# Gated DeltaNet layer: joins on both column halves, a raised eviction rank, another spread of the gates, outputs turned by VectorE

## The chip, the cores and the metric

The kernel runs on one core of a Trainium2 chip. The metric is the device time of one execution in microseconds (us). The five engines have a queue each and meet by semaphores: TensorE (PE, with its weight loads PEld), VectorE (DVE), ScalarE (ACT), GpSimd (POOL), and SyncE (SP), which issues the DMAs.

## The reference

Four layers over 1024 positions of width 1024, each with RMSNorm, adaLN shift and scale, one input projection that also gives a SiLU gate, a mixer, an output projection and a gated residual. The mixers are HGRN2, sliding-window attention, gated DeltaNet (GDN), HGRN2. All is fp32. The change is in the GDN layer (one helper of the HGRN2 layers is renamed):

```python
def gdn_mixer(h, w_in, w_out, conv_w, a_log, dt_bias, onorm_g):
    qkv, z, a, b = jnp.split(h @ w_in, [GD_QKV, GD_QKV + GD_VW, GD_QKV + GD_VW + GD_V_HEADS], axis=-1)
    qkv = jax.nn.silu(causal_conv(qkv, conv_w))
    ...
    beta = jax.nn.sigmoid(b)
    g = -jnp.exp(a_log) * jax.nn.softplus(a + dt_bias)
    o = gated_delta_scan(q, k, v, beta, g)
    o = rmsnorm(o, onorm_g).reshape(B, T, GD_VW)
    return (o * jax.nn.silu(z)) @ w_out
# gated_delta_scan, for each chunk:
    X = lax.linalg.triangular_solve(A + eye, rhs, left_side=True, lower=True, unit_diagonal=True)
    u, w = X[..., :dv], X[..., dv:]
    v_new = u - w @ S
    o = (q_ * jnp.exp(d)[..., None]) @ S + qk @ v_new
    S = S * jnp.exp(d_last) + (k_ * jnp.exp(d_last - d)[..., None]).T @ v_new
```

There are 8 key heads and 16 value heads of 128. z is the gate, a and b give the decays.

## The kernel before

Activations lie with features on the 128 partitions and time in two halves (hf) of 512. An fp32 operand is split in a high and a low part, and each product is three matmuls (mm3, L195 to L197): hi by hi, lo by hi, hi by lo. proj_fm projects 128 columns so (24 matmuls per half) and gives the PSUM bank to an eviction (evac).

The GDN layer goes by u = 0 to 7, a key head with its two value heads. proj_kq evicts k and q with a short convolution (conv: copy gd_xs L627, first tap L631, three taps on DVE L633, tanh L634, product L635). proj_v does the same for v and turns it with PE (vtr_ps). proj_z evicts the gates (L709, L711) and stores them in the DRAM tensor od[1], where the outputs later stand too. inverse(u) inverts the 16 triangular matrices of 128 of a pair: 62 substitution steps on DVE for blocks of 32 (L766, L767), joins of 32 (z_ps L795, L805, L806), then two joins of 64 (L814, L821), each 16 products of 64 by 64, with copies by ACT and DVE after each. Both joins of 64 take one half of PE's columns: the first puts its results on partitions 64 to 127 (up) of two PSUM banks, the second on 0 to 63 (lo).

scan(u) goes through 8 chunks of 128 in order with the state S: ks_ps (L864, L865), y on DVE (L870), w_ps (L875), ws on ACT (L876) and wg on DVE (L877), the new state (S_ps L881, DVE L887), and the output product w_ps L891, added to ot (L894). After four chunks finish normalizes: it multiplies ot by the factor of each row (L842), turns it in four PE transposes (otr_ps L845), multiplies by the gate loaded from od[1] (L847) and stores it there. out_load later loads the outputs and splits them (o_hi on ACT, o_lo on DVE, L1182, L1183), and out_mm multiplies them by the output weights (outp_ps).

The order of the work is fixed when the program is built. weave merges generators by planned time: for each pair scan(u) and inverse(u+1) lie beside a chain of projections for later pairs, and the table ZL says which gates are projected beside which pair. high_priority ranks instructions within a scheduler that then writes one fixed in-order queue for each engine; burst gives a rank of 4000, which keeps a group of matmuls together. The first inverse has a weave of its own, beside kq of u = 1, v of u = 0 and the second half of u = 0's gates. Ahead of it the first half of the projection for u = 0 runs under early, with a raised rank, while the norm of the second half (hhi L496) is still being made. decays projects a and b with weights gd_wab split in hi and lo, 32 columns each.

Of the kernel before, what the change touches and what calls it, by code (L numbers as in the profile page):

```python
# [10 lines left out]
F32 = mybir.dt.float32  # L11
# [9 lines left out]
P = 128  # L21
T = 1024
# [9 lines left out]
GB = {"k": 5, "q": 4, "kt": 4, "v": 4, "zs": 1, "tmp": 2, "tb": 3, "of": 2, "f256": 4, "ot": 1}  # L32
# [3 lines left out]
EO, EW = 60, 150  # L36
# [10 lines left out]
ZL = ((1, 0, 1), (2, 0, 1)), ((3, 0, 1),), ((4, 0, 1),), ((5, 0),), ((5, 1),), ((6, 0, 1),), ((7, 0, 1),), ()  # L47
# [36 lines left out]
class Trunk:  # L84
    def __init__(self, ctx, tc, ins):
# [8 lines left out]
        self.np_, self.pb, self.pw = 0, 3, 0  # L94
        self.dram = pool("dram", space=bass.MemoryType.DRAM)
        self.xd = self.dram.tile([D, T], F32, name="xd")
        self.od = [self.dram.tile([D * (1 + n), T], F32, name=f"od{n}") for n in range(2)]
        self.hhi, self.hlo = [None, None], [None, None]
# [14 lines left out]
    def early(self, g):  # L113

        self.pw = EW
        with self.tc.high_priority(offset=EO):
            drain(g)
        self.pw = 0
# [14 lines left out]
    def burst(self):  # L133

        return self.tc.high_priority(offset=BURST)

# [363 lines left out]
    def proj_fm(self, w, c0, evac, halves=(0, 1)):  # L500

        w = self.pre.pop(c0, None) or self.load_cols(w, c0)
        for hf in halves:
# [6 lines left out]
            evac(hf, ps)  # L510
# [14 lines left out]
    def gdn(self, i, side):  # L525
# [88 lines left out]
        place = lambda h, hf: self.od[1][h * P:(h + 1) * P, hf * HT:(hf + 1) * HT]  # L614
# [90 lines left out]
        def proj_z(u, dd, halves=(0, 1)):  # L705
            for a in range(2):
                def ev(hf, ps):
                    th = tl("tb")
                    nc.scalar.activation(th, ps, AF.Tanh, scale=0.5)  # L709
                    zs = tl("zs")  # L710
                    nc.vector.scalar_tensor_tensor(zs, th, 1.0, ps, ALU.add, ALU.mult)  # L711
# [762 lines left out]
```

## Time and profile before

| | us |
|---|---|
| runs | 2743.67, 2731.29, 2732.64 |
| median | 2732.64 |
| the profiled execution's own time | 2734.63 |
| span of its profile | 2732.9 |

The profile is of one execution. Its page gives busy times by engine, a chain of work traced back from the end, and the costliest groups of instructions; other views of the trace give single instructions, waits by releaser, and windows. Matmuls run in a pipeline and their ends are modelled, so a matmul's price is read from the spacing of starts, not from its duration. Among the largest groups of the page are, beside the projections, these rows of the GDN layer (busy us, mean ns | idle before them and what ended it):

```profile
L633 DVE SCALAR_TENSOR_TENSOR gd_tb<-gd_xs,taps,gd_tb 128x512 f32<-128x512 f32 x192 | 144.9, 754 | 22.5 <-ACT gd_tb L631 20.1
```

### The profile page before, as it was taken

How to read it: one execution, taken by the hardware profiler on the slowest of the kernel's cores; microseconds unless marked ns; L12 is line 12 of the kernel's file. 1: busy time of each engine (PE TensorE's matmuls, PEld its weight loads, DVE VectorE, ACT ScalarE, POOL GpSimd, SP SyncE). 2: the span in 40 equal slices, each digit the busy share in tenths (PEclk: the TensorE clock that was granted, in tenths of full speed). 3: DMA queues.
4: the chain of work that ended last, by engine and by line, in shares of the span. 5: the costliest groups of instructions: out<-in, count | busy, mean ns of one | idle time of the engine just before them, and what ended most of it. 6: DMA issues, size and time to landing. Idle time of an engine off the chain costs nothing.

```text
span 2732.9 us, 51521 instructions
## 1 busy us (share of the span) xinstructions
PE 2647.5 (97%) x19071; PEld 2133.6 (78%) x19071; DVE 2019.3 (74%) x5714; ACT 1235.5 (45%) x3139; POOL 132.6 (5%) x352
## 2 busy tenths in 40 slices
PE   8999999999999999899999999999999999999999
PEld 4878878778877767677788887788778888887877
DVE  6776766778687877677888898988765857556575
ACT  4333333444454655454456456555543433333342
POOL 0000100000000000001001100100000001000000
PEclk9999999999999999999999999999999999999999
DMA  6332222344223243324343344332553211111133
GB/s 238 97 94 78 67 81 79 113 133 148 65 83 97 91 141 100 110 70 115 101 124 102 97 125 112 103 103 77 151 189 117 78 58 38 55 44 47 46 121 113
DMA packets 347665, 273.29 MB, mean 100 GB/s; under 512 B 68963, under 2 KB 276246, under 8 KB 347414
## 3 DMA queue, kind: packets, MB, share of 16 engines
q1 hardware_dynamic: 347126, 268.95, 32.8%
q8 instruction: 150, 2.46, 0.4%
q14 instruction: 101, 0.83, 0.1%
q0 software_dynamic: 288, 1.05, 0.1%
HBM read 224.77 MB, written 45.15 MB: 99 GB/s over the span
## 4 chain that ended last, share of the span: by engine, by line
PE 73%; DVE 15%; DMA 6%; ACT 3%; issue 2%; SPq 0%; DVEq 0%; ACTq 0%
PE proj_ps L196 10%; PE proj_ps L195 10%; PE proj_ps L197 10%; PE outp_ps L195 4%; PE outp_ps L197 4%; PE outp_ps L196 4%; DMA ada_w<-in_ada_w_dram 3%; PE projt_ps L195 3%; PE projt_ps L197 3%; PE projt_ps L196 3%; DVE w_lo L171 1%; PE pv_ps L1356 1%; DVE gd_tb L633 1%; PE ada_row L391 1%; PE w_ps L875 1%
## 5 line engine op out<-in xcount | busy, mean ns | idle before, releaser
L195 PE MATMUL proj_ps<-hhi,w_hi 128*128 128x512 f32 x1664 | 679.9, 409 | 12.6 <-ACT gd_tb L631 11.4
L197 PE MATMUL proj_ps<-hhi,w_lo 128*128 128x512 f32 x1664 | 680.5, 409 | 0.0
L196 PE MATMUL proj_ps<-hlo,w_hi 128*128 128x512 f32 x1664 | 675.2, 406 | 0.0
L195 PEld LDWEIGHTS proj_ps<-hhi,w_hi 128*128 128x128 f32 x1664 | 316.2, 190 | 71.1 <-ACT gd_tb L631 15.6
L196 PEld LDWEIGHTS proj_ps<-hlo,w_hi 128*128 128x128 f32 x1664 | 315.8, 190 | 58.6 <-issue 2.4
L197 PEld LDWEIGHTS proj_ps<-hhi,w_lo 128*128 128x128 f32 x1664 | 315.9, 190 | 56.4 <-issue 1.0
L170 ACT CAST w_hi<-w_raw 128x512 fp32r<-128x512 f32 x332 | 201.9, 611 | 309.3 <-PE proj_ps L196 195.0
L171 DVE TENSOR_TENSOR w_lo<-w_raw,w_hi 128x512 fp32r<-128x512 f32 x332 | 223.4, 675 | 158.2 <-ACT w_hi L170 132.5
L196 PE MATMUL projt_ps<-w_lo,hhi 128*128 128x256 f32 x896 | 258.7, 291 | 4.7 <-DVE w_lo L171 4.7
L195 PE MATMUL projt_ps<-w_hi,hhi 128*128 128x256 f32 x896 | 257.7, 290 | 0.9 <-ACT w_hi L170 0.9
L197 PE MATMUL projt_ps<-w_hi,hlo 128*128 128x256 f32 x896 | 256.8, 290 | 0.0
L195 PE MATMUL outp_ps<-o_hi,w_hi 128*128 128x512 f32 x576 | 229.2, 400 | 3.8 <-ACT o_hi L1182 2.4
L196 PE MATMUL outp_ps<-o_lo,w_hi 128*128 128x512 f32 x576 | 229.2, 399 | 0.0
L197 PE MATMUL outp_ps<-o_hi,w_lo 128*128 128x512 f32 x576 | 227.9, 398 | 0.8 <-DVE w_lo L174 0.8
L196 PEld LDWEIGHTS projt_ps<-w_lo,hhi 128*128 128x128 f32 x896 | 171.1, 192 | 8.1 <-DVE w_lo L171 6.0
L195 PEld LDWEIGHTS projt_ps<-w_hi,hhi 128*128 128x128 f32 x896 | 171.1, 192 | 4.0 <-ACT w_hi L170 1.3
L197 PEld LDWEIGHTS projt_ps<-w_hi,hlo 128*128 128x128 f32 x896 | 170.8, 192 | 2.3 <-issue 1.0
L633 DVE SCALAR_TENSOR_TENSOR gd_tb<-gd_xs,taps,gd_tb 128x512 f32<-128x512 f32 x192 | 144.9, 754 | 22.5 <-ACT gd_tb L631 20.1
L173 ACT ACTIVATE w_hi<-w_raw,par 128x512 fp32r<-128x512 f32 (+1 forms) x136 | 94.5, 698 | 140.0 <-PE outp_ps L196 98.9
L195 PEld LDWEIGHTS outp_ps<-o_hi,w_hi 128*128 128x128 f32 x576 | 108.8, 189 | 27.7 <-ACT o_hi L1182 3.8
L174 DVE SCALAR_TENSOR_TENSOR w_lo<-w_raw,par,w_hi 128x512 fp32r<-128x512 f32 (+1 forms) x136 | 96.8, 716 | 43.5 <-ACT w_hi L173 42.4
L404 DVE SCALAR_TENSOR_TENSOR ada_acc<-ada_w,par,ada_acc 128x512 f32<-128x512 f32 x140 | 104.5, 746 | 32.4 <-DMA ada_w<-in_ada_w_dram 31.4
(394 smaller groups left out, 4918.9 us busy)
## 6 DMA issues: line engine op xcount, KB each, us to landing
ada_w<-in_ada_w_dram SPq DMA_DIRECT2D x160, 256.0 KB, 2.7
w_raw<-in_hg_in_w_dram SPq DMA_DIRECT2D x136, 256.0 KB, 2.8
w_raw<-in_gd_in_w_dram SPq DMA_DIRECT2D x108, 256.0 KB, 3.1
o_in<-od SPq DMA_DIRECT2D x72, 256.0 KB, 3.2
w_raw<-in_gd_out_w_dram SPq DMA_DIRECT2D x64, 256.0 KB, 2.8
w_raw<-in_sw_in_w_dram SPq DMA_DIRECT2D x48, 256.0 KB, 2.9
w_raw<-in_hg_out_w_dram SPq DMA_DIRECT2D x40, 256.0 KB, 2.8
ada_w<-in_ada_w_dram SPq DMA_DIRECT2D x8, 1024.0 KB, 9.0
```

Source lines behind the costliest of these rows:

```text
L170: nc.scalar.copy(hi, raw)
L171: nc.vector.tensor_tensor(lo, raw, hi.bitcast(F32), ALU.subtract)
L173: nc.scalar.activation(hi, raw, AF.Copy, scale=scale)
L174: nc.vector.scalar_tensor_tensor(lo, raw, scale, hi.bitcast(F32), ALU.mult, ALU.subtract)
L195: mm(out, a[0], b[0], start=start, stop=False)
L196: mm(out, a[0], b[1], start=False, stop=False)
L197: mm(out, a[1], b[0], start=False, stop=stop)
L391: nc.tensor.matmul(pr[0:1, :], self.cT[:, k:k + 1], wk[:, k, :], start=k == 0, stop=k == KT - 1)
L404: self.nc.vector.scalar_tensor_tensor(acc, w, c, acc, ALU.mult, ALU.add)
L633: nc.vector.scalar_tensor_tensor(y, xs[:, j:j + HT], w(j), y, ALU.mult, ALU.add)
L875: nc.tensor.matmul(po[:, hd[a]], dd["u"][a, hf][:, cs], rhs, start=True, stop=True)
L1356: nc.tensor.matmul(po[a * 64:(a + 1) * 64], vg[:, n + 1 - nkb + b, :], p4[:, :, a, :], start=b == 0, stop=b == nkb - 1)
```

## The change

Six things are changed.

- early takes a rank (EV = 300) for the evictions of the first projection.
- decays has the high and low columns of a and b side by side as 64 columns: two matmuls per block in place of three. The two halves of the result are added after the transposes, by an ACT copy and a DVE add. The product lo by lo is now computed too.
- In inverse the joins of 64 go by turns to both column halves of PE, in one bank. Bursts are tied, so that all wait for the first. The joins of 32 are in another order, and two of the four POOL copies stand later.
- The first weave has the projections in another order, with the gates of u = 1, and 72.8 us of planned work; ZL is shifted by one pair.
- finish has no PE transposes and no gate: the multiply by the row's factor writes in a permuted order, a DVE transpose turns blocks of 32 by 32, and four DMAs store the result. The gates have their own DRAM tensor zd and are multiplied in out_load, on DVE.
- In scan wg is computed by ACT, after the S_ps matmuls.

Lines in the changed kernel are 9 to 18 further on (L627 is L644, L766 is L782, L821 is L836, L891 is L906).

**The start of the layer, ACT.** hhi is the normed input of the second half, gd_xs the copy that begins an eviction of the first projections, gd_wab the weights of a and b. Before:

```order
L170 CAST w_hi<-w_raw 128x512
L496 ACTIVATE hhi<-n_t,mod 128x512 x2
L170 CAST w_hi<-w_raw 128x512
L496 ACTIVATE hhi<-n_t,mod 128x512 x2
L627 COPY gd_xs<-proj_ps 128x512
L631 ACTIVATE gd_tb<-proj_ps,taps 128x512
L544 CAST gd_wab<-w_raw 128x256
L627 COPY gd_xs<-proj_ps 128x512
L575 ACTIVATE gd_tmp<-gd_tmp 128x16
```

With the change:

```order
L179 CAST w_hi<-w_raw 128x512
L505 ACTIVATE hhi<-n_t,mod 128x512 x2
L179 CAST w_hi<-w_raw 128x512
L505 ACTIVATE hhi<-n_t,mod 128x512 x2
L644 COPY gd_xs<-proj_ps 128x512
L648 ACTIVATE gd_tb<-proj_ps,taps 128x512
L644 COPY gd_xs<-proj_ps 128x512
L555 CAST gd_wab<-w_raw 128x8x32
L592 ACTIVATE gd_tmp<-gd_tmp 128x16
```

The first eviction stands in the same place; the second has moved ahead of the cast of gd_wab.

**The first inverse, DVE.** L766 and L767 (later L782, L783) are the substitution, one pair for each j. Before, from the fifth pair:

```order
L766 TENSOR_TENSOR gd_tmp<-gd_A,gd_Tb 128x81
L767 TENSOR_TENSOR gd_Tb<-gd_Tb,gd_tmp 128x27x3
L766 TENSOR_TENSOR gd_tmp<-gd_A,gd_Tb 128x78
L677 TENSOR_SCALAR gd_ms<-gd_ms 128x16
L767 TENSOR_TENSOR gd_Tb<-gd_Tb,gd_tmp 128x26x3
L150 TENSOR_SCALAR rs_y<-gd_ms 128x16
L766 TENSOR_TENSOR gd_tmp<-gd_A,gd_Tb 128x100
L152 SCALAR_TENSOR_TENSOR rs_t<-rs_y,gd_ms 128x16
L633 SCALAR_TENSOR_TENSOR gd_tb<-gd_xs,taps,gd_tb 128x512
L767 TENSOR_TENSOR gd_Tb<-gd_Tb,gd_tmp 128x25x4
L153 TENSOR_TENSOR rs_t<-rs_t,rs_y 128x16
L633 SCALAR_TENSOR_TENSOR gd_tb<-gd_xs,taps,gd_tb 128x512
```

With the change, from the second half of the second pair's rows:

```order
L727 SCALAR_TENSOR_TENSOR gd_tb<-gd_tb,proj_ps 128x512
L783 TENSOR_TENSOR gd_Tb<-gd_Tb,gd_tmp 128x30
L782 TENSOR_TENSOR gd_tmp<-gd_A,gd_Tb 128x58
L783 TENSOR_TENSOR gd_Tb<-gd_Tb,gd_tmp 128x29x2
L782 TENSOR_TENSOR gd_tmp<-gd_A,gd_Tb 128x56
L783 TENSOR_TENSOR gd_Tb<-gd_Tb,gd_tmp 128x28x2
L782 TENSOR_TENSOR gd_tmp<-gd_A,gd_Tb 128x81
L783 TENSOR_TENSOR gd_Tb<-gd_Tb,gd_tmp 128x27x3
L782 TENSOR_TENSOR gd_tmp<-gd_A,gd_Tb 128x78
L783 TENSOR_TENSOR gd_Tb<-gd_Tb,gd_tmp 128x26x3
L782 TENSOR_TENSOR gd_tmp<-gd_A,gd_Tb 128x100
L783 TENSOR_TENSOR gd_Tb<-gd_Tb,gd_tmp 128x25x4
```

Taps of convolutions (L633) and the norm of the next k and q (L677, L150 to L154) stood between the steps; now a few evictions of gates (L727) do, and some rows further on weights (w_lo).

**The last scan, PE.** This is behind the last join of 64. proj_ps are the last projections, outp_ps the output projection; S_ps, ks_ps and w_ps are the scan of u = 7. Before, from the second product of its first chunk on:

```order
L875 MATMUL w_ps<-gd_v,gd_uq 128x128
L196 MATMUL outp_ps<-o_lo,w_hi 128x512
L197 MATMUL outp_ps<-o_hi,w_lo 128x512
L195 MATMUL outp_ps<-o_hi,w_hi 128x512
L881 MATMUL S_ps<-gd_ws,gd_kt 128x256
L891 MATMUL w_ps<-gd_wg,gd_uq 128x128 x2
L196 MATMUL outp_ps<-o_lo,w_hi 128x512
L197 MATMUL outp_ps<-o_hi,w_lo 128x512
L864 MATMUL ks_ps<-gd_S,gd_k 128x256
L865 MATMUL ks_ps<-gd_S,gd_q 128x256
```

With the change, the rows from the first new state on:

```order
L895 MATMUL S_ps<-gd_ws,gd_kt 128x256
L906 MATMUL w_ps<-gd_wg,gd_uq 128x128
L206 MATMUL proj_ps<-hhi,w_lo 128x512
L906 MATMUL w_ps<-gd_wg,gd_uq 128x128
L879 MATMUL ks_ps<-gd_S,gd_k 128x256
L880 MATMUL ks_ps<-gd_S,gd_q 128x256
L890 MATMUL w_ps<-gd_y,gd_uq 128x128 x2
L895 MATMUL S_ps<-gd_ws,gd_kt 128x256
L906 MATMUL w_ps<-gd_wg,gd_uq 128x128 x2
L879 MATMUL ks_ps<-gd_S,gd_k 128x256
L880 MATMUL ks_ps<-gd_S,gd_q 128x256
L658 MATMUL vtr_ps<-ident,gd_tb 128x128 x4
```

Before, output rows (outp_ps) stood around the first steps of the scan; now two steps follow each other with transposes of v alone between them. Between the last join and the first outp_ps stand 36 proj_ps rows before, 13 with the change.

The diff, cut where it repeats itself:

```diff
-GB = {"k": 5, "q": 4, "kt": 4, "v": 4, "zs": 1, "tmp": 2, "tb": 3, "of": 2, "f256": 4, "ot": 1}
+GB = {"k": 5, "q": 4, "kt": 4, "v": 4, "tmp": 2, "tb": 4, "of": 2, "f256": 4, "ot": 1}
...
-EO, EW = 60, 150
+EO, EW, EV = 60, 150, 300
...
-ZL = ((1, 0, 1), (2, 0, 1)), ((3, 0, 1),), ((4, 0, 1),), ((5, 0),), ((5, 1),), ((6, 0, 1),), ((7, 0, 1),), ()
+ZL = ((2, 0, 1),), ((3, 0, 1),), ((4, 0, 1),), ((5, 0, 1),), ((6, 0),), ((6, 1),), ((7, 0, 1),), ()
...
-    def early(self, g):
-        self.pw = EW
+    def early(self, g, pe=0):
+        self.pw, self.pe = EW, pe
...
-        self.pw = 0
+        self.pw = self.pe = 0
...
+    def tied(self, mms):
+        with self.burst():
+            first = mms[0]()
+            with self.tc.issue_after(first.ins):
+                for m in mms[1:]:
+                    m()
...
-            evac(hf, ps)
+            with self.tc.high_priority(offset=self.pe):
+                evac(hf, ps)
+                n = self.tc.cur_priority
+            self.tc.cur_priority = n + self.pe
...
-        wv = gp.tile([P, 4, KT, 32], F32R, name="gd_wab", tag="blk", bufs=1)
-        wab = [wv[:, 0], wv[:, 1]]
+        wab = gp.tile([P, 2 * KT, 64], F32R, name="gd_wab", tag="blk", bufs=1)[:, :KT, :]
...
-        nc.scalar.copy(wab[0], raw)
-        nc.vector.tensor_tensor(wab[1], raw, wab[0].bitcast(F32), ALU.subtract)
+        nc.scalar.copy(wab[:, :, 0:32], raw)
+        nc.vector.tensor_tensor(wab[:, :, 32:64], raw, wab[:, :, 0:32].bitcast(F32), ALU.subtract)
...
         def decays():
...
-            abT = gp.tile([P, T], F32, name="gd_abT", tag="blk", bufs=1)[:32]
+            abT = gp.tile([P, T], F32, name="gd_abT", tag="blk", bufs=1)[:64]
             for hf in range(2):
-                ps = self.proj_ps("ab_ps")
-                for k in range(KT):
-                    self.mm3(ps[:32, :], (wab[0][:, k, :], wab[1][:, k, :]), (self.hhi[hf][:, k, :], self.hlo[hf][:, k, :]), k == 0, k == KT - 1)
-                nc.scalar.copy(abT[:, hf * HT:(hf + 1) * HT], ps[:32, :])
+                ps = self.proj_ps("ab_ps")[:64]
+                with self.burst():
+                    for k in range(KT):
+                        nc.tensor.matmul(ps, wab[:, k, :], self.hhi[hf][:, k, :], start=k == 0, stop=False)
+                        nc.tensor.matmul(ps, wab[:, k, :], self.hlo[hf][:, k, :], start=False, stop=k == KT - 1)
+                nc.scalar.copy(abT[:, hf * HT:(hf + 1) * HT], ps)
...
-                nc.tensor.transpose(pt[:, c * 32:(c + 1) * 32], abT[:, c * P:(c + 1) * P], self.ident[:32, :32])
-            pab = pt[:, :256].rearrange("p (c n) -> p n c", c=C)
+                nc.tensor.transpose(pt[:, c * 64:(c + 1) * 64], abT[:, c * P:(c + 1) * P], self.ident[:64, :64])
...
+            p4, ab2 = pt.rearrange("p (c b n) -> p b c n", c=C, b=2), par[:, 2 * P:].rearrange("p (c n) -> p c n", c=C)
+            nc.scalar.copy(ab2, p4[:, 1])
+            nc.vector.tensor_tensor(ab2, ab2, p4[:, 0], ALU.add)
+            pab = ab2.rearrange("p c n -> p n c")
...
                 def ev(hf, ps):
...
-                    zs = tl("zs")
-                    nc.vector.scalar_tensor_tensor(zs, th, 1.0, ps, ALU.add, ALU.mult)
-                    nc.sync.dma_start(place(2 * u + a, hf), zs)
+                    nc.vector.scalar_tensor_tensor(th, th, 1.0, ps, ALU.add, ALU.mult)
+                    nc.sync.dma_start(place(self.zd, 2 * u + a, hf), th)
...
-            for b in range(4):
+            for b in (2, 3):
...
-            with self.burst():
-                for g in range(N):
-                    for z, p_, b_ in ((za, 0, 1), (zb, 2, 3)):
-                        nc.tensor.matmul(z[R[p_], g, :], Z[R[b_], g, 0:32], Uc[R[b_], g, :], start=True, stop=True)
-                    nc.tensor.matmul(za[R[1], g, :], Uc[R[1], g, :], Z[R[1], g, 0:32], start=True, stop=True)
+            self.tied([f for g in range(N) for f in (
+                lambda g=g: nc.tensor.matmul(zb[R[2], g, :], Z[R[3], g, 0:32], Uc[R[3], g, :], start=True, stop=True),
+                lambda g=g: nc.tensor.matmul(za[R[0], g, :], Z[R[1], g, 0:32], Uc[R[1], g, :], start=True, stop=True),
+                lambda g=g: nc.tensor.matmul(za[R[1], g, :], Uc[R[1], g, :], Z[R[1], g, 0:32], start=True, stop=True))])
...
+            nc.vector.tensor_copy(uv[R[2], :, R[3]], zb[R[2]])
...
-            nc.vector.tensor_copy(uv[R[2], :, R[3]], zb[R[2]])
...
-            zs = [bank("z_ps", 64) for _ in range(2)]
-            with self.burst():
-                for g in range(N):
-                    nc.tensor.matmul(zs[g // 8][up, g % 8, :], uv[lo, g, up], Z[lo, g, :], start=True, stop=True)
-            nc.scalar.copy(Z[up, 0:8], zs[0][up])
-            nc.vector.tensor_copy(Z[up, 8:16], zs[1][up])
-            yield 1800
-            zs = [bank("z_ps", 64) for _ in range(2)]
-            with self.burst():
-                for g in range(N):
-                    nc.tensor.matmul(zs[g // 8][lo, g % 8, :], Z[up, g, :], uv[up, g, up], start=True, stop=True)
-            nc.scalar.copy(uv[lo, 0:8, up], zs[0][lo])
-            nc.vector.tensor_copy(uv[lo, 8:16, up], zs[1][lo])
-            yield 1800
+            z = bank("z_ps", 64)
+            self.tied([lambda g=g, q=q: nc.tensor.matmul(z[q, g % 8, :], uv[lo, g, up], Z[lo, g, :], start=True, stop=True)
+                       for n in range(8) for g, q in ((n, up), (n + 8, lo))])
+            for b in (0, 1):
+                nc.gpsimd.tensor_copy(uv[R[b], :, R[b]], Uc[R[b]])
+            nc.scalar.copy(Z[up, 0:8], z[up])
+            nc.vector.tensor_copy(Z[up, 8:16], z[lo])
+            yield 900
+            z = bank("z_ps", 64)
+            self.tied([lambda g=g, q=q: nc.tensor.matmul(z[q, g % 8, :], Z[up, g, :], uv[up, g, up], start=True, stop=True)
+                       for n in range(8) for g, q in ((n + 8, up), (n, lo))])
+            nc.scalar.copy(uv[lo, 0:8, up], z[lo])
+            nc.vector.tensor_copy(uv[lo, 8:16, up], z[up])
+            yield 900
...
-            of = [tl("of") for a in range(2)]
-            for a in range(2):
-                nc.sync.dma_start(of[a], place(2 * u + a, hf))
...
             for a in range(2):
-                ov = ot[:, :, a * P:(a + 1) * P]
-                nc.vector.tensor_tensor(ov, ov, f[:, a, :, None].to_broadcast([P, NC, P]), ALU.mult)
-                pt = self.psum("ta", "otr_ps", 1)
-                for c in range(NC):
-                    nc.tensor.transpose(pt[:, c * P:(c + 1) * P], ot[:, c, a * P:(a + 1) * P], self.ident)
-                yield 436
-                nc.vector.tensor_tensor(of[a], pt, of[a], ALU.mult)
-                nc.sync.dma_start(place(2 * u + a, hf), of[a])
+                ov = ot[:, :, a * P:(a + 1) * P].rearrange("p c (b r) -> p c b r", b=4)
+                on, ob = tl("of"), tl("of")
+                nc.vector.tensor_tensor(on.rearrange("p (b c r) -> p c b r", b=4, c=NC), ov, f[:, a, :, None, None].to_broadcast([P, NC, 4, 32]), ALU.mult)
+                nc.vector.transpose(ob, on)
+                dst = place(od, 2 * u + a, hf).rearrange("(b q) (d t) -> d q b t", b=4, d=4)
+                for d in range(4):
+                    nc.sync.dma_start(dst[d], ob[d * 32:(d + 1) * 32].rearrange("q (b t) -> q b t", b=4))
+                yield 1
...
                     nc.scalar.activation(ws[:, hd[a]], po[:, hd[a]], AF.Copy, scale=col(dd["gw"], a, n))
-                    nc.vector.tensor_scalar(wg[:, hd[a]], po[:, hd[a]], col(dd["gm"], a, n), None, ALU.mult)
...
+                    nc.scalar.activation(wg[:, hd[a]], po[:, hd[a]], AF.Copy, scale=col(dd["gm"], a, n))
...
-        self.early(proj_kq(0, ds[0], ((0,),)))
+        self.early(proj_kq(0, ds[0], ((0,),)), EV)
...
-        weave(self.tc, (inverse(0, ds[0]), 28000, 0, 1, 100), (chain(proj_kq(1, ds[1]), proj_v(0, ds[0]), proj_z(0, ds[0], (1,))), 52000, 0, 1, 0))
+        weave(self.tc, (inverse(0, ds[0]), 28000, 0, 0.8, 100),
+              (chain(proj_z(0, ds[0], (1,)), proj_v(0, ds[0]), proj_z(1, ds[1]), proj_kq(1, ds[1])), 72800, 0, 1, 0))
...
-                cs += [self.out_load(od, 0, KT, 0, gp, "tmp", 2), self.out_mm(i, w_out, 0, KT, 0, on), self.out_load(od, 0, KT, 1, gp, "tmp", 2)]
+                cs += [self.out_load(od, 0, KT, 0, gp, "tmp", 2, (self.zd, "tb", bufs["tb"])), self.out_mm(i, w_out, 0, KT, 0, on), self.out_load(od, 0, KT, 1, gp, "tmp", 2, (self.zd, "tb", bufs["tb"]))]
...
             nc.sync.dma_start(t, od[(k0 + k) * P:(k0 + k + 1) * P, sl])
+            if gates:
+                zd, ztag, znb = gates
+                z = pool.tile([P, HT], F32, name="o_z", tag=ztag, bufs=znb)
+                nc.sync.dma_start(z, zd[(k0 + k) * P:(k0 + k + 1) * P, sl])
+                v4 = lambda x, o: x.rearrange(f"p ({o} r) -> p c a r", c=NC, a=4)
+                nc.vector.tensor_tensor(v4(z, "c a"), v4(t, "a c"), v4(z, "c a"), ALU.mult)
+                t = z
```

More of the change, by code (lines that the diff above doesn't have):

```diff
@@ L93, in __init__ @@
         self.ps = pool("ps", space=PSUM)
-        self.np_, self.pb, self.pw = 0, 3, 0
+        self.np_, self.pb, self.pw, self.pe = 0, 3, 0, 0
         self.dram = pool("dram", space=bass.MemoryType.DRAM)
@@ L612, in gdn @@
         col = lambda a, h, c: a[:, h * C + c:h * C + c + 1]
-        place = lambda h, hf: self.od[1][h * P:(h + 1) * P, hf * HT:(hf + 1) * HT]
+        place = lambda d, h, hf: d[h * P:(h + 1) * P, hf * HT:(hf + 1) * HT]
         Z = gp.tile([P, 16, 64], F32, name="gd_Z")
@@ L932, in gdn @@
         self.fill_x(1)
-        yield chain(self.out_mm(i, w_out, 0, KT, 1, on), self.out_load(od, KT, KT, 0, tp, "o_in", 3),
-                    self.out_mm(i, w_out, KT, KT, 0, on), self.out_load(od, KT, KT, 1, tp, "o_in", 3))
+        yield chain(self.out_mm(i, w_out, 0, KT, 1, on), self.out_load(od, KT, KT, 0, tp, "o_in", 3, (self.zd, "o_z", 3)),
+                    self.out_mm(i, w_out, KT, KT, 0, on), self.out_load(od, KT, KT, 1, tp, "o_in", 3, (self.zd, "o_z", 3)))
         yield self.out_mm(i, w_out, KT, KT, 1, on)
@@ L1024, in mm @@
                         return nc.tensor.matmul(pl[gs, n, c * 48:(c + 1) * 48], k[:, c * P + g * 32:c * P + (g + 1) * 32], x[:, 4 * c + g, :], start=True, stop=True)
-                    todo = [(n, c, g) for n in range(len(xks)) for c in range(NC) for g in range(4)]
-                    with self.burst():
-                        first = mm(*todo[0])
-                        with self.tc.issue_after(first.ins):
-                            for m in todo[1:]:
-                                mm(*m)
+                    self.tied([lambda n=n, c=c, g=g: mm(n, c, g) for n in range(len(xks)) for c in range(NC) for g in range(4)])
                     return pl
@@ L1172, in proj_tm, with out_load @@
             evac(tp, ps)
-    def out_load(self, od, k0, nk, hf, pool, tag, nb):
+    def out_load(self, od, k0, nk, hf, pool, tag, nb, gates=None):
         nc = self.nc
```

1 line of the change is left out of this document (added).

## Prediction

> **What bounds the kernel now.** I read the page first, then the windows of the stage that the change touches, then the waits of TensorE (PE) in it. The page's engine rows and its chain by engine:
>
> ```profile
> PE 2647.5 (97%) x19071; PEld 2133.6 (78%) x19071; DVE 2019.3 (74%) x5714; ACT 1235.5 (45%) x3139; POOL 132.6 (5%) x352
> ...
> PE 73%; DVE 15%; DMA 6%; ACT 3%; issue 2%; SPq 0%; DVEq 0%; ACTq 0%
> ```
>
> PE works 97% of the span and carries the chain, so a matmul taken away is time taken away, unless PE then waits. Where it may wait is read by stage. The columns of windows are the stretch and its length, then busy time (and count) of PE, weight loads, VectorE (DVE), ScalarE (ACT), POOL, then PE's granted clock, DMA share and GB/s. The gated DeltaNet layer (GDN) runs from about 1110 to 2178 us: first projections and first inverse until 1280, head pairs until 1930, the last scan until 2050.
>
> ```profile
> 1130.00:1160.00 30.00, 22.42 (x96) 13.41 (x96) 14.94 (x24) 13.36 (x37) 2.79 (x11) 0.89 0.31 87
> 1190.00:1220.00 30.00, 26.06 (x115) 20.41 (x114) 21.34 (x55) 15.08 (x49) 1.23 (x6) 0.94 0.32 80
> 1220.00:1250.00 30.00, 25.10 (x109) 19.35 (x109) 28.96 (x95) 15.90 (x42) 3.07 (x4) 0.92 0.31 88
> 1280.00:1930.00 650.00, 640.19 (x4355) 518.36 (x4354) 571.43 (x1689) 354.54 (x1112) 46.29 (x129) 1.00 0.38 105
> 1930.00:2050.00 120.00, 117.71 (x729) 93.29 (x728) 86.33 (x189) 59.69 (x148) 4.04 (x8) 0.96 0.55 175
> 1940.00:1950.00 10.00, 10.00 (x68) 8.21 (x66) 5.17 (x10) 2.06 (x4) 0.00 (x0) 0.58 0.11 31
> ```
>
> In the long middle PE is busy 640 of 650 us, though DVE works 571 us beside it (88%). In the first stage PE stands idle and its clock falls: the three 30 us rows leave 16.4 us without a matmul. The end has one dip, clock 0.58 over 10 us, about 4 us lost. PE's waits by releaser (total, times, longest), first from 1110 to 1280, then, behind the dots, the largest of the middle:
>
> ```profile
> PE proj_ps L195 <- ACT gd_tb L631: 10.0, 4, 6.0
> PE vtr_ps L641 <- DVE gd_tb L635: 3.7, 1, 3.7
> PE ab_ps L195 <- DVE gd_zs L711: 1.3, 1, 1.3
> ...
> PE z_ps L814 <- DVE gd_uq L809: 2.0, 3, 0.9
> ```
>
> So the middle pays for matmuls, the first stage also for waits.
>
> **Output transposes (finish).** These rows go, 128 matmuls in bursts of four:
>
> ```profile
> L845 PE MATMUL otr_ps<-ident,gd_ot 128*128 128x128 f32 x128 | 20.4, 283 | 0.8 <-DVE gd_ot L842 0.4
> 1309.85 0.60 PE L845 MATMUL otr_ps<-ident,gd_ot 128*128 128x128 f32 x4
> ```
>
> Matmuls overlap, so the price is the spacing: (0.60 - 0.28) / 3 = 0.107 us, times 128 = **-13.7 us**, all on PE's path. DVE takes over the turn:
>
> ```profile
> L842 DVE TENSOR_TENSOR gd_ot<-gd_ot,gd_f 128x512 f32<-128x512 f32 x32 | 21.1, 684 | 0.1
> L847 DVE TENSOR_TENSOR gd_of<-otr_ps,gd_of 128x512 f32<-128x512 f32 x32 | 22.0, 687 | 5.7 <-PE otr_ps L845 4.5 <-DMA w_raw<-in_gd_out_w_dram 0.7
> L422 DVE STREAM_TRANSPOSE ada_t<-ada_acc 128x512 f32<-128x512 f32 x20 | 14.1, 705 | 0.2
> L877 DVE TENSOR_SCALAR gd_wg<-w_ps,gd_gm 128x128 f32<-128x128 f32 x128 | 44.5, 347 | 15.0 <-ACT gd_ws L876 13.8
> L876 ACT ACTIVATE gd_ws<-w_ps,gd_gw 128x128 f32<-128x128 f32 x128 | 47.2, 369 | 43.8 <-PE w_ps L875 42.9
> L980 DVE TENSOR_TENSOR hg_qf<-hg_q,hg_f 128x256 f32<-128x256 f32 x32 | 13.7, 427 | 0.0
> L894 DVE TENSOR_TENSOR gd_ot<-w_ps,gd_qse 128x256 f32<-128x256 f32 x56 | 23.4, 418 | 2.3 <-PE w_ps L891 1.9
> ```
>
> Of the 64 rows L842 and L847, L842 stays with a permuted output, L847 goes, a 32x32 turn of 0.705 us comes (L422 is this operation at this size), and the gate multiply comes back in the output loads, 32 x 0.69 = 22 us; L877 leaves DVE for ACT. In the scans DVE gets -44.5 - 22.0 + 22.6 = -44 us, ACT about 128 x 0.37 = +47 us. No row has the permuted write. L980 reads with a stride and takes 427 ns beside 418 ns of L894 at the same size, so I take 0.69 us; bounds 0.69 and, if four pieces of a quarter cost as four L877 each, 1.4 us. On PE's path this costs **0** in the middle: its cover is that DVE and ACT have less or little to do there (571 - 44 and 355 + 47 of 650 us). Behind the moved wg stand ACT's next evictions, and the w_ps matmuls of L891 wait for it; projection rows stand around them, except at the end (below). Stores: 128 of 64 KB in place of 32 of 256 KB, and the gate loads move from finish to the output loads; DMA share is 0.38 in the middle, so 0.
>
> **Joins of 64 (inverse).** Both column halves are used in turn, in one PSUM bank. Each fp32 product is two records:
>
> ```profile
> L821 PE MATMUL z_ps<-gd_uq,gd_Z 64*64 64x64 f32 x256 | 19.2, 232 | 0.0
> L814 PE MATMUL z_ps<-gd_Z,gd_uq 64*64 64x64 f32 x256 | 19.0, 225 | 4.6 <-DVE gd_uq L809 3.5 <-ACT gd_Z L807 1.1
> 1559.94 2.08 PE L821 MATMUL z_ps<-gd_uq,gd_Z 64*64 64x64 f32 x32
> 151.28 0.55 PE L1024 MATMUL lev_ps<-hg_X,hg_kg 128*32 128x48 f32 x32
> ```
>
> Sixteen products lie (2.08 - 0.23) / 31 = 60 ns a record apart. The HGRN burst L1024 alternates four column groups on the same rows: 0.55 / 32 = at most 17 ns a record, where 48 columns at the joins' rate would be 45. Different columns thus overlap; two halves should give 30 ns. 512 records x 30 ns = **-15.4 us**; bounds 0 (no overlap) and 512 x (60 - 17) = -22. I take the half, since two groups can at best halve. A rule speaks against it. The Trainium skill, page "TensorE: Matmul & The Clock Gate", section "Part 3: Packing small matmuls — row/col tiling", says that a weight load overlaps matmuls in flight only where its row group differs. The pairs here share their rows, so by that rule this term would be 0; the L1024 row, same rows and other columns, disagrees with it. Between the two joins 4 to 11 projection rows now stand in the order, and these cover the copies.
>
> **Decays.** 48 matmuls become 32:
>
> ```profile
> 1143.39 0.39 PE L196 MATMUL ab_ps<-hlo,gd_wab 128*32 128x512 f32 x1
> 1143.62 0.39 PE L197 MATMUL ab_ps<-hhi,gd_wab 128*32 128x512 f32 x1
> ```
>
> 16 x 0.23 = **-3.7 us**. The extra ACT copy and DVE add delay the inverse by about 1 us; projections run meanwhile: 0.
>
> **Evictions above the norm.** PE's 6.0 us wait is this (ACT rows: start, duration, last the PE row that waited):
>
> ```profile
> 1133.48 1.38 ACT L496 ACTIVATE hhi<-n_t,mod 128x512 fp32r<-128x512 f32 x2 [0.84 <-DVE n_t L495]
> 1134.76 0.57 ACT L627 COPY gd_xs<-proj_ps 128x512 f32<-128x512 f32 x1
> 1135.23 0.69 ACT L631 ACTIVATE gd_tb<-proj_ps,taps 128x512 f32<-128x512 f32 x1
> ...
> 1135.97 0.79 PE L195 MATMUL proj_ps<-hhi,w_hi 128*128 128x512 f32 x1 [5.96 <-ACT gd_tb L631]
> ```
>
> ACT runs the second half's hhi ahead of the first eviction. In the order of the changed kernel the first gd_xs copy still stands behind all of them; only the second moved up by a row. So **0**; bound -6 if the wait went, +1 if the moved cast delays the decays.
>
> **First weave.** The same projections in another order over 72.8 us of planned work. In the two 30 us rows from 1190 PE lacks 8.8 us and the clock costs (0.06 + 0.08) x 30 = 4 us. DVE is 97% busy in the second: it runs the substitution.
>
> ```profile
> 1218.36 0.18 DVE L766 TENSOR_TENSOR gd_tmp<-gd_A,gd_Tb 128x31 f32<-128x31 f32 x1
> ...
> 1252.38 0.17 DVE L766 TENSOR_TENSOR gd_tmp<-gd_A,gd_Tb 128x16 f32<-128x16 f32 x1
> ```
>
> These 62 steps take 34 us, since convolutions stand between them; in the new order mostly gate evictions do. But no DVE work disappears: the convolutions of v now crowd ahead of it, those of kq(1) behind. I take a third of the 12.8 us: **-4**, bounds -12 and +3 (one more wait like the 3.7 us above).
>
> **End of the layer.** After the last join the old order has 36 projection rows ahead of the first output row, the new one 13, since gates and projections were spent earlier. Two steps of the scan then stand without cover. What such a step costs is seen once in the middle:
>
> ```profile
> 1731.77 0.48 PE L197 MATMUL proj_ps<-hhi,w_lo 128*128 128x512 f32 x1
> ...
> 1735.74 0.67 PE L864 MATMUL ks_ps<-gd_S,gd_k 128*128 128x256 f32 x2 [0.49 <-DVE gd_Tb L767]
> ```
>
> From the end of the former to the start of the latter are 3.5 us for about 1 us of matmul: 2.5 us lost. Two make +5; the eight slices of the first output load now take two DVE passes, 8 x 0.69 = +5.5 us ahead of the first output matmuls. Against it I set the dip's 4 us, whose joins now have projections between them: **+6**, bounds -2 and +14.
>
> **Sum.** -13.7 - 15.4 - 3.7 + 0 - 4 + 6 = -30.8 us. The profiled execution took 2734.6 us (span 2732.9), 2.0 above the median 2732.6; so 2734.6 - 30.8 - 2.0 = **2702 us**.
>
> **Rivals.** R1, the column halves don't overlap: 2702 + 15 = 2717; against it stands the L1024 row, for it the page's rule. R2, the first stage loses all its waits and dips (-12 for -4) and the end costs 2 or 3 us: 2691; for it the lighter substitution, against it DVE's load. R3, the eviction does get ahead of hhi, in time if not in the order: 2696; the order speaks against it. R4, the slower side: the permuted multiplies (32 in finish, 32 in the output loads) cost far more than 0.69 us. At 2.2 us each they add 32 x 1.5 = 48 us to the scans, which takes back the 44 and holds DVE at 93% of a shortened middle, where I let 20 us of PE's gain be lost, and 16 x 1.5 = 24 us in the loads of the end, on the path, and 5 for dips of the clock: -31 + 44 + 5 = +18, so 2734.6 + 18 - 2 = 2751. It decides from about 1.7 us each; L980 speaks against it. R5, matmuls saved but not time: DVE at 88% and the serial inverse and scan set the middle, PE waits instead, and the end costs its upper bound: -31 + 20 + 8, about 2730. For it: at 1731.77 PE already waited so; against it: 9 us of waits in 650.
>
> **How the numbers follow.** Forecast 0.53, R1 0.12, R2 0.15, R3 0.05, R4 0.05, R5 0.10. Range 2684 to 2724: it takes in R1 to R3 and the bounds around them and leaves out R4, R5 and the tails of both, under 0.2. About 0.5% is what a measurement of this kernel can tell from no change: below 2719 is faster, above 2746 slower. Forecast, R2, R3 and half of R1 give 0.8 faster; R5, the other half, and a little of the rest 0.14; R4 and its like 0.06.
>
> **What would show it.** No L845 rows; the z_ps bursts of 64 near 1.1 us for 32 records (2 us is R1); the wait of 6 us still at 1130 to 1136; the DVE multiplies of finish near 0.7 us (over 1.7 is R4); PE still over 97% busy between 1280 and 1900 (if under 96%, R5); waits of about 10 us after the last join. Wrong it would be through the unpriced permuted write, or if the new order of the first stage starves PE.

## The result and the profile after

| | us |
|---|---|
| runs with the change | 2695.95, 2691.39, 2692.61, 2694.55, 2694.46 |
| median (before: 2732.64) | 2694.46 |
| ratio to before, 95% interval | 0.9863, [0.9848, 0.9878] |
| span of the profiled execution (before: 2732.9) | 2694.2 |

The change takes 38 us off; the forecast was 31 us, in a range of 2684 to 2724. The engine rows and the chain of the page after:

```profile
PE 2609.7 (97%) x18927; PEld 2102.4 (78%) x18927; DVE 2010.2 (75%) x5619; ACT 1272.9 (47%) x3268; POOL 136.7 (5%) x352
...
PE 71%; DVE 17%; DMA 5%; ACT 3%; issue 3%; SPq 1%; POOL 0%; DVEq 0%; ACTq 0%; POOLq 0%
```

TensorE (PE) lost 38 us of busy time and the span 39 us: it still is the bound. VectorE (DVE) gave up 9 us over the whole kernel and ScalarE (ACT) took 37 more. Groups of instructions after, by line (columns as in the page's part 5):

```profile
L828 PE MATMUL z_ps<-gd_Z,gd_uq 64*64 64x64 f32 x256 | 10.3, 232 | 6.6 <-DVE gd_uq L823 6.6
L836 PE MATMUL z_ps<-gd_uq,gd_Z 64*64 64x64 f32 x256 | 10.0, 232 | 0.1
L858 DVE TENSOR_TENSOR gd_of<-gd_ot,gd_f 128x512 f32<-128x512 f32 x32 | 22.1, 690 | 0.3
L859 DVE STREAM_TRANSPOSE gd_of<-gd_of 128x512 f32<-128x512 f32 x32 | 22.5, 704 | 0.1
L1198 DVE TENSOR_TENSOR o_z<-o_in,o_z 128x512 f32<-128x512 f32 x32 | 21.8, 687 | 9.6 <-DMA o_z<-zd 6.6 <-issue 1.4 <-DMA o_in<-od 1.2
```

The joins of 64 fell from 19.0 + 19.2 to 10.3 + 10.0 us, each record about as long as before (225 and 232 ns): their spacing shrank. PE now waits 6.6 us in sum ahead of them, 4.6 before. One burst in the timeline:

```profile
1539.24 1.15 PE L836 MATMUL z_ps<-gd_uq,gd_Z 64*64 64x64 f32 x32
```

(1.15 - 0.23) / 31 = 30 ns a record, where it was 60. The permuted multiplies, 0.690 and 0.687 us, cost what the plain ones cost (0.684 and 0.687). The windows of the stages (columns as in the prediction):

```profile
1130.00:1160.00 30.00, 22.05 (x94) 14.87 (x93) 18.04 (x31) 15.45 (x42) 2.92 (x10) 0.89 0.26 71
1190.00:1220.00 30.00, 30.00 (x143) 24.34 (x142) 26.44 (x70) 17.16 (x43) 1.51 (x6) 1.00 0.35 92
1220.00:1250.00 30.00, 28.97 (x209) 23.39 (x210) 23.30 (x63) 11.17 (x28) 4.08 (x10) 1.00 0.50 126
1250.00:1280.00 30.00, 28.40 (x266) 22.92 (x256) 17.91 (x31) 16.02 (x56) 2.82 (x6) 0.83 0.19 51
1280.00:1900.00 620.00, 608.48 (x4219) 487.45 (x4218) 548.45 (x1601) 383.11 (x1219) 51.16 (x129) 1.00 0.38 99
```

From 1190 to 1250 PE idles 1 us where it idled 8.8, and the clock is full; a new dip, a stretch at a lower granted clock, stands from 1250 on (0.83). The middle is as full as it was (98%). PE's waits, 1120 to 1290 and behind the dots 1900 to 2100:

```profile
PE proj_ps L204 <- ACT gd_tb L648: 5.9, 1, 5.9
PE ab_ps L575 <- DVE gd_tb L727: 2.0, 1, 2.0
...
PE S_ps L895 <- ACT gd_ws L891: 1.0, 2, 0.5
PE w_ps L890 <- ACT gd_ws L891: 1.0, 2, 0.5
PE w_ps L890 <- DVE gd_y L885: 0.9, 1, 0.9
PE w_ps L906 <- ACT gd_wg L905: 0.7, 2, 0.5
PE outp_ps L204 <- ACT o_hi L1200: 0.4, 1, 0.4
```

The wait at the start is still there, 5.9 us. The last scan waits in many small pieces, none over 1 us. The first output matmul starts behind the first of the eight multiplies of its output load, and the last of the eight comes 12 us later:

```profile
1927.34 0.68 DVE L1198 TENSOR_TENSOR o_z<-o_in,o_z 128x512 f32<-128x512 f32 x1
1929.88 0.80 PE L204 MATMUL outp_ps<-o_hi,w_hi 128*128 128x512 f32 x1 [0.36 <-ACT o_hi L1200]
1942.11 0.69 DVE L1198 TENSOR_TENSOR o_z<-o_in,o_z 128x512 f32<-128x512 f32 x1
```

By stage. The bounds are rows of PE: the start runs from n_rb of the second half to the last ab_ps, the first weave from there to the first S_ps, the middle to the first row of the last pair of joins of 64, the end to the last outp_ps. Some stages now hold more or fewer projection rows; the last column prices each of these at its spacing of 0.23 us and takes it out:

| stage | before | after | projection rows | change at equal work |
|---|---|---|---|---|
| start | 36.1 | 33.1 | same | -3.0 |
| first weave | 121.7 | 116.5 | +12 | -8.0 |
| middle | 660.6 | 638.1 | +7 | -24.1 |
| end | 219.7 | 209.9 | -19 | -5.4 |

In another profile of the same program (e5, below) the last column is -1.0, -12.5, -25.8 and -4.1, so a stage read from one profile is good to a few us only.

### The profile page after: what moved, and what is told of

The parts are those of the page before. It is cut to its first block, busy times and chain, and to the rows that moved or that the text cites. A ratio compares the mean times of both kernels' runs of the same rounds, so it can differ in the third digit from the quotient of the medians.

```text
span 2694.2 us, 51458 instructions
## 1 busy us (share of the span) xinstructions
PE 2609.7 (97%) x18927; PEld 2102.4 (78%) x18927; DVE 2010.2 (75%) x5619; ACT 1272.9 (47%) x3268; POOL 136.7 (5%) x352
## 4 chain that ended last, share of the span: by engine, by line
PE 71%; DVE 17%; DMA 5%; ACT 3%; issue 3%; SPq 1%; POOL 0%; DVEq 0%; ACTq 0%; POOLq 0%
PE proj_ps L206 10%; PE proj_ps L205 9%; PE proj_ps L204 9%; PE outp_ps L204 5%; PE outp_ps L205 5%; PE outp_ps L206 5%; DMA ada_w<-in_ada_w_dram 3%; PE projt_ps L204 3%; PE projt_ps L206 3%; PE projt_ps L205 3%; DVE w_lo L180 2%; DVE gd_tb L650 2%; PE pv_ps L1374 1%; DVE ada_acc L413 1%; PE w_ps L890 1%
## 5 line engine op out<-in xcount | busy, mean ns | idle before, releaser
L206 PEld LDWEIGHTS outp_ps<-o_hi,w_lo 128*128 128x128 f32 x576 | 108.7, 189 | 23.5 <-DVE w_lo L183 1.3
```

Of the source, the lines that this page charges most:

```text
L206: mm(out, a[1], b[0], start=False, stop=stop)
```

## The experiments

Each run was compared with the kernel before on the same chip. The control, e5, is the changed kernel unedited. The ratios, with 95% intervals:

| run | median us | ratio to before |
|---|---|---|
| e1, joins not by turns | 2699.99 | 0.9891 [0.9866, 0.9915] |
| e2, old first weave and table | 2697.24 | 0.9877 [0.9856, 0.9898] |
| e3, outputs turned by PE | 2698.88 | 0.9889 [0.9867, 0.9911] |
| e4, wg on DVE | 2700.11 | 0.9894 [0.9869, 0.9919] |
| e5, control | 2692.18 | 0.9863 [0.9848, 0.9877] |
| e6, norm behind the eviction | 2690.49 | 0.9860 [0.9837, 0.9882] |
| e7, three tiles | 2686.80 | 0.9845 [0.9826, 0.9864] |
| e8, e6 and the last gates divided | 2696.55 | 0.9875 [0.9860, 0.9890] |
| e9, before, gates in place | 2731.84 | 0.9999 [0.9985, 1.0014] |
| e10, e6 and three tiles | 2685.96 | 0.9839 [0.9820, 0.9858] |
| e11, before, joins alone | 2709.28 | 0.9926 [0.9905, 0.9947] |
| e12, no rank | 2690.76 | 0.9854 [0.9835, 0.9873] |

The runs e1 to e4 were on one chip, e5 to e8 on a second, e9 to e12 on a third. The kernel before took 2729.2 to 2730.5 us (medians) on all three, but the control ran on the second alone, so for the others a difference from it is one between chips. Apart from e9 and e11, every interval above overlaps the control's: a difference of 4 to 8 us is likely, and settled only where a trace shows it too.

**The control.**

> The changed kernel itself, on the chip and beside the runs of the next three, so that they are compared at the same place. All theories: a ratio of about 0.986 to the kernel before.

The ratio is that of the first measurement to four digits. Its profiled span is 2689.6, though, against 2694.2 of the same program: single profiles differ by 5 us. So ratios are compared below, and profiles say where a difference lies.

**The turns of the joins.** The sixteen products of a join go first to one column half, then to the other.

```diff
-   for n in range(8) for g, q in ((n, up), (n + 8, lo))])
+   for g, q in [(n, up) for n in range(8)] + [(n + 8, lo) for n in range(8)]])
```

and likewise in the second join.

> The changed kernel, with the sixteen products of each join of 64 in another order: eight on one column half, then eight on the other, where the change goes by turns. Every queue has otherwise the same rows. Theory (the gain of the joins is the overlap of the two column halves): a burst of 32 records goes back from 1 us to about 2 us, 512 records x 30 ns = 15 us, so about 2710 us against 2694.5. Rival (a load can't overlap a product on the same rows, and the gain came from the single bank and the tied burst): bursts and time stay, 2694.

A burst, in the timeline of e1:

```profile
1538.80 1.90 PE L836 MATMUL z_ps<-gd_uq,gd_Z 64*64 64x64 f32 x32
```

It is back near 2 us, and the queues have the same rows but for this order. The order of the column halves alone makes the difference, and the overlap is shown. The groups of the two joins:

```profile
L828 PE MATMUL z_ps<-gd_Z,gd_uq 64*64 64x64 f32 x256 | 16.5, 232 | 6.6 <-DVE gd_uq L823 6.6
L836 PE MATMUL z_ps<-gd_uq,gd_Z 64*64 64x64 f32 x256 | 15.3, 222 | 0.0
```

That is 11.5 us more busy time than in the change, not 15, since here too the halves meet once in each burst: where one half follows the other, three pairs of records start 4 to 6 ns apart, most others some 58. The ratio gives 0.0028 x 2730 = 7.6 us over the control, with intervals that overlap: the direction is the theory's, the size half of its.

**The joins alone.** The kernel before with the inverse of the change from its second burst on, and nothing else: joins of 64 by turns and tied, joins of 32 in the new order, two POOL copies later.

> The kernel before with the inverse of the change alone: joins of 64 by turns on both column halves, in one bank, tied, joins of 32 in the new order, two POOL copies later. Theory (a burst shorter is time less): bursts of 64 shrink by 15 us in sum and the time by 11 to 16 us, 2714 to 2719. Rival (the chain of inverse and scan on VectorE fills what the bursts leave, as undoing the turns alone cost 7 us for 11 us of bursts): 5 to 8 us less than before.

0.9926 is 20 us, 14 to 26 by its interval, where the theory said 11 to 16 and the rival 5 to 8. The windows of e11:

```profile
1190.00:1220.00 30.00, 26.36 (x124) 20.90 (x123) 23.14 (x64) 15.72 (x56) 0.73 (x4) 1.00 0.31 80
1220.00:1250.00 30.00, 25.78 (x108) 20.05 (x107) 27.16 (x86) 14.56 (x34) 3.07 (x4) 0.89 0.37 110
...
1280.00:1900.00 620.00, 607.96 (x4260) 490.92 (x4260) 558.25 (x1646) 342.14 (x1076) 49.41 (x126) 1.00 0.39 108
1900.00:2020.00 120.00, 118.51 (x766) 93.83 (x765) 90.87 (x213) 64.61 (x168) 5.76 (x11) 1.00 0.56 172
```

By the bounds of the stage table the middle takes 647.5 us, before 660.6, with the same projection rows to one, and DVE is at 90% in the 620 us above: DVE does not hold PE back there. PE's idle time from 1190 to 1250 is nearly as before (7.9 us, 8.8 before). The clock dip behind the last join is gone (1.00 in the last row), which is a part of what goes beyond the bursts' own 15 us.

**The turn of the outputs.** finish and the output loads as before, the gates in zd. The diff shows one place of it:

```diff
...
-                nc.vector.transpose(ob, on)
+                for c in range(NC):
+                    nc.tensor.transpose(pt[:, c * P:(c + 1) * P], ot[:, c, a * P:(a + 1) * P], self.ident)
...
```

> The changed kernel with finish as before: four transposes on TensorE per head and half, and the gates multiplied there; the output loads are plain. Theory (the transposes stood on TensorE's path): 128 x 0.102 = +13 us, about 2707 us. Rival (VectorE is the bound of the middle, and taking 22 us of output-load multiplies away pays as much as the transposes cost): 2694 to 2700.

7 us over the control (0.0026 x 2730), between theory and rival, with intervals that overlap. 128 transposes are back on PE, yet the end no longer waits for the scan's small steps: of PE's waits from 1900 to 2100 only two are left.

```profile
PE vtr_ps L658 <- DVE gd_tb L652: 0.9, 1, 0.9
PE otr_ps L861 <- DVE gd_ot L858: 0.3, 1, 0.3
```

PE is busy 118.6 of the 120 us from 1900 to 2020, in the change 115.5. So the transposes filled gaps there that they leave open when they go.

**wg on ACT.**

```diff
-                    nc.scalar.activation(wg[:, hd[a]], po[:, hd[a]], AF.Copy, scale=col(dd["gm"], a, n))
+                    nc.vector.tensor_scalar(wg[:, hd[a]], po[:, hd[a]], col(dd["gm"], a, n), None, ALU.mult)
```

with the second line at its old place, beside ws.

> The changed kernel with wg of the scan computed by VectorE as before, in place of ScalarE. Theory (covered by projections in the middle): within 2 us of 2694.5, and TensorE's waits in the middle stay under 15 us. Rival (VectorE's 44 us are what let the middle keep pace with a shorter TensorE): 5 to 15 us slower, 2700 to 2710, with VectorE over 93% busy.

0.0031 x 2730 = 8.5 us over the control: the rival in time, with DVE busy 523.6 of the 570 us between 1280 and 1850, 92% and not over 93, where the control has 507.7, 89%. Most of the loss sits in one place, in e4's timeline and windows:

```profile
1910.75 1.12 PE L658 MATMUL vtr_ps<-ident,gd_tb 128*128 128x128 f32 x4 [4.16 <-DVE gd_tb L652]
```

```profile
1900.00:1930.00 30.00, 21.04 (x274) 16.76 (x273) 18.04 (x32) 12.60 (x29) 3.81 (x8) 0.66 0.53 156
```

The last convolution of v comes late from DVE, PE waits 4 us, and a long stretch at half clock (0.66 over the 30 us; the control has 0.89 there) lies over the joins. It is no accident of this profile: all four runs of e4 were granted a mean clock of 0.987 to 0.990, the control's 0.991 to 0.993. DVE's relief is worth that much at the end of the pairs, and it was priced at nothing.

**The first weave.** The weave's chain, with its planned work, and ZL as before.

> The changed kernel with the first weave and the table of the gates as before. Theory (the new order of the first stage gains 7 to 9 us, and the end loses little): 2694.5 + 6 = about 2700 us, with waits of TensorE for convolutions back between 1200 and 1250. Rival from the prediction (first stage -4, end +6): undoing both gives 2692, a little faster than the change.

4 us over the control by the ratios, between theory and rival, intervals overlapping. Few of the waits on evictions came back: 8.2 us on gd_tb with 6.0 of it in the first one, where the kernel before has 10.0 + 3.7 + 2.2. So the order of the projections is not what took most of the waits out of the first stage. What it does change is the substitution on DVE, 34 us before, here from 1213.5 to 1248.7, but with the change from 1213.7 to 1235.7:

```profile
1213.72 0.19 DVE L782 TENSOR_TENSOR gd_tmp<-gd_A,gd_Tb 128x31 f32<-128x31 f32 x1
...
1235.51 0.17 DVE L782 TENSOR_TENSOR gd_tmp<-gd_A,gd_Tb 128x16 f32<-128x16 f32 x1
```

An inverse that is done 12 us earlier hardly shortened the stage: PE is full of projections there, and at equal work the first weave is 11.5 us shorter than before in e2 and 12.5 in the control.

**What emptied it.** First, one tile less (`"tb": 4` to `"tb": 3`).

> The changed kernel with three in place of four of the tiles in which evictions work (gd_tb); nothing else. Theory (the first stage gains by the fourth tile and not by the order of the projections, since the old order gave back only 2 to 3 us): waits of TensorE on evictions come back between 1155 and 1280, 4 to 8 us more than the control. Rival (the fourth tile only replaces the tile of the gates that was removed): within 2 us of the control.

The rival, no loss, and rather a gain: 0.0018 x 2730 = 5 us less than the control, intervals overlapping. Then the gates in place, in the kernel before:

```diff
-                    zs = tl("zs")
-                    nc.vector.scalar_tensor_tensor(zs, th, 1.0, ps, ALU.add, ALU.mult)
-                    nc.sync.dma_start(place(2 * u + a, hf), zs)
+                    nc.vector.scalar_tensor_tensor(th, th, 1.0, ps, ALU.add, ALU.mult)
+                    nc.sync.dma_start(place(2 * u + a, hf), th)
```

> The kernel before with one edit: the gates are evicted in place, in four gd_tb tiles, and the single gd_zs tile is gone (as in the change); they are still stored in the tensor of the outputs and multiplied in finish. Theory (in the first stage TensorE waited because gate evictions queued for the one gd_zs tile and its store): the waits of the first stage between 1157 and 1280 fall from 11 to under 5 us and its half clock goes, 6 to 10 us less than before, about 2722. Rival (the first stage gains by something else of the change, since three tiles in place of four made no difference): within 3 us of before.

The time is the rival's, the place is the theory's. The windows of e9:

```profile
1190.00:1220.00 30.00, 26.80 (x125) 21.22 (x124) 23.08 (x61) 16.09 (x54) 1.10 (x6) 1.00 0.36 88
1220.00:1250.00 30.00, 29.49 (x136) 23.12 (x135) 28.94 (x94) 16.58 (x44) 2.19 (x4) 1.00 0.24 72
...
1280.00:1900.00 620.00, 609.10 (x4155) 495.31 (x4153) 540.04 (x1577) 336.23 (x1056) 49.88 (x126) 0.98 0.38 104
```

The 3.7 us wait and both dips of the first stage are gone. From 1157 to 1290 PE waits 4.3 us, before 9.2; its waits for ACT's evictions to gd_tb stay (3.2 us, before 4.0). In this execution the middle pays it back: a clock of 0.98 over 620 us is 12 us, and before it was 1.00. Whether the edit brings these dips or chance does, one profile can't tell. The gate tile was the cause of about half of the first stage's waits; curing it alone is worth nothing in the ten runs.

**The wait at the start.** The main part of the edit:

```diff
...
+            if self.late:
+                late, self.late = self.late, None
+                with self.tc.issue_after(e.ins):
+                    self.norm_apply(*late, tl=tl)
...
```

in conv, behind the first tap; the norm of the second half is no longer applied ahead of the layer.

> The changed kernel with the application of the second half's norm written behind the first eviction of k, and its ScalarE rows (hhi) tied behind that eviction; its temporaries lie in tiles of the layer's own pool. Now the eviction really stands ahead of the norm in ScalarE's queue. Theory (the 6 us wait and the half clock behind it come from ScalarE's order alone): the wait of 5.9 us goes, and 6.8 us at half clock with it, so 6 to 9 us less than the control. Rival (the norm of the second half is itself what is late, TensorE then waits for hhi or hlo instead): no gain, a new wait of 4 us or more before 1160.

The eviction now stands ahead of the norm and the time is the control's. PE's rows at that place in e6, then DVE's:

```profile
1131.68 1.09 PE L663 MATMUL ktr_ps<-ident,gd_k 128*128 128x128 f32 x4 [5.97 <-DVE gd_k L657]
```

```profile
1120.94 0.75 DVE L655 SCALAR_TENSOR_TENSOR gd_tb<-gd_xs,taps,gd_tb 128x512 f32<-128x512 f32 x1
1121.60 1.41 DVE L507 SCALAR_TENSOR_TENSOR hlo<-gd_tmp,mod,hhi 128x512 fp32r<-128x512 f32 x2
1122.93 1.40 DVE L505 SCALAR_TENSOR_TENSOR gd_tmp<-x,gcol,n_rb 128x512 f32<-128x512 f32 x2
1124.24 0.75 DVE L655 SCALAR_TENSOR_TENSOR gd_tb<-gd_xs,taps,gd_tb 128x512 f32<-128x512 f32 x1
...
1130.85 0.69 DVE L657 SCALAR_TENSOR_TENSOR gd_k<-gd_tb 128x512 f32<-128x512 f32 x1
```

The wait of 6 us changed its name: PE's transposes of k wait for the convolution, whose four DVE rows stand one by one among the norm's. It was never ACT's order alone; DVE has the norm and the convolution to do at once.

That the edit is worth nothing is not shown by this, though. The four runs of e6 were granted a mean clock of 0.987 to 0.991, the control's 0.991 to 0.993; between the means lie 0.003, which is at most 8 us of 2690. In e6's windows:

```profile
1725.00:1745.00 20.00, 18.53 (x215) 15.27 (x216) 15.24 (x38) 8.75 (x21) 4.52 (x8) 0.74 0.19 43
1905.00:1925.00 20.00, 16.17 (x204) 13.62 (x201) 14.14 (x26) 10.91 (x30) 1.88 (x2) 0.74 0.63 193
```

The control has a clock of 1.00 and 0.91 there. So the edit may have gained a few us that half clock over later joins took back; no run parts the two.

**The rank.** EV taken away.

> The changed kernel without the rank for the first evictions. TensorE's queue has the same rows; on ScalarE one eviction stands one row later, on VectorE two convolution taps change places with the split of gd_wab. Theory: no difference, a ratio of 0.985 to 0.988 like the control, the wait of 5.9 us the same. Rival: the wait grows by about 1 us and the time by 1 to 3 us.

No difference, as PE's unchanged queue says.

**The end.** `((7, 0, 1),), ()` becomes `((7, 0),), ((7, 1),)` in ZL, in the kernel of e6.

> The kernel of e6 with the gates of the last pair divided: one half beside pair 6, the other beside pair 7, so that the last scan has 48 more projection rows beside it. Theory (bare steps of the last scan cost some us): 2 to 5 us less than e6, with TensorE's waits behind the last join gone. Rival (the wait moves: pair 6 lacks the rows, or the output loads come later): within 2 us of e6 or slower.

The rival: 0.0015 x 2730 = 4 us slower than e6, intervals overlapping. PE now waits for the output loads (1.9 us for o_lo, 1.3 for o_hi), so more cover for the scan's steps is no gain.

**Three tiles in e6.**

> The kernel of e6 with three gd_tb tiles as in e7. Theory (both differences are the noise of single half-clock stretches, a few us each): a ratio between 0.984 and 0.987, not to be told from the control. Rival (both are real and add up): 0.983 or less, about 2684.

The lowest median here, 2685.96; its runs (2684.96 to 2687.34) lie below those of the control (2691.32 to 2695.07), but the intervals of the ratios overlap. That it beats the change by some 6 us is likely and not settled, since the two ran on different chips; e12, on the chip of e10 and with the control's PE queue, took 2688.03 to 2691.33. No run here says why fewer tiles should help.

## Why the prediction was right, and where it was not

The direction, the bound and the large terms were right. With a join's pair priced at 15.4 / 8 = 1.9 us (one pair in the first weave, six in the middle, one in the end) and 104 of the 128 transposes in the middle, 24 in the end, the forecast by stage is this:

| stage | forecast | measured at equal work |
|---|---|---|
| start | -3.7 | -3.0 |
| first weave | -4 - 1.9 = -5.9 | -8.0 |
| middle | -11.6 - 11.1 = -22.7 | -24.1 |
| end | +6 - 1.9 - 2.6 = +1.5 | -5.4 |

- **PE bounds, so a matmul taken away is time.** Held, most plainly in e11.
- **Joins, -15.4.** Groups: 38.2 to 20.3 us, -17.9; in both profiles some of it lies at half clock, and the control, whose joins do not, has 18.7. The 30 ns a record came out exactly. The rule of the Trainium skill (page "TensorE: Matmul & The Clock Gate", section "Part 3: Packing small matmuls — row/col tiling") that a load overlaps only where its row group differs gives the wrong forecast here: e1 and the change have the same rows of the array in each burst and differ only in the order of the columns, 1.90 against 1.15 us. R1 fell.
- **Transposes, -13.7.** The rows went, and the middle is as much shorter as joins and transposes together were to make it. But undoing it costs only 7 us in e3, about half: some of the rows stood in gaps of the last scan, and e3 gives the gate multiply back to finish too.
- **Permuted multiplies at 0.69 us.** 0.690 and 0.687. R4 fell by its condition, the price.
- **Decays, -3.7.** The start is 3.0 us shorter in this profile.
- **Rank, 0, with the wait of 6 us staying.** Held (5.9 us; e12), and R3 fell. The reason given, that the eviction stands behind hhi in ACT's order, was only half of it: e6 put it ahead, and the wait moved to DVE's rows.
- **First weave, -4, and R2.** The stage lost nearly all its waits, and the end cost less than forecast: that is R2, at 2691, as much as the forecast, at 2702; the measured 2694.5 lies between. The reason that R2 gave, the lighter substitution, came true (34 to 22 us) without being what paid: in e2 the substitution is as long as before, and the stage at equal work nearly as short as in the control. About half of the waits went with the gate tile (e9), which the prediction saw only as a renamed buffer.
- **ACT's wg, 0.** "On PE's path this costs 0" holds for ACT, but DVE's side was put at nothing, and this step failed: by e4 (intervals overlapping) it is worth some 8 us, because DVE's last convolution of v comes in time.
- **DVE at 88%, R5.** PE is 98% busy from 1280 to 1900, so R5 fell.
- **End, +6.** This term was mis-sized. The 5.4 us, less 1.9 for the joins and 2.6 for the transposes, leave about -1 for it. Two of its three pieces held: the two bare steps cost PE 2.3 and 1.4 us of waits, priced at 2.5 each, and the dip behind the last join went (a clock of 0.99 from 1900 to 2020, before 0.96). What failed is the +5.5 us for eight DVE passes ahead of the first output matmuls: the first of them needs one slice and waited 0.4 us, and the other passes ran while PE worked.

The sum fell 7 us short of the gain in the medians, 10 in this table of one profile. By the table most of that lies in the end, where the output loads were priced as a delay that did not come.

The single terms do not add up: undoing one part costs 4 to 8 us each (e1 to e4), 27 us together, and one part alone gave 20 (e11) or none (e9). It looks as if what one part frees another fills; no run shows this by itself.

## What to carry to other kernels

Small matmuls that use half of the array's columns are worth ordering by turns over the column halves: here the same instructions took about half the time. A wait of an in-order engine is cured only if the next releaser in line is early too: put the row ahead, and read which engine the wait names then. Before a load in slices is priced as a delay, ask what its first user needs: here one slice of eight.

## What was not expected of the hardware

Half clock can cost more than the wait that it comes with: in e4 a wait of 4.16 us (to 1910.75) runs into a stretch of 20.5 us at half clock (from 1908.1), in which PE worked 13.7 us, so about 7 us were lost. And one program does not always dip at the same places: the changed kernel's first profile has a clock of 0.83 from 1250 to 1280, the control's 1.00 there. That alone is up to 0.17 x 30 = 5 us, as much as their spans differ.
